# Packing the small constants of a one-core decoder layer, so that its large tiles start elsewhere in the on-chip memory

## The chip, the cores and the metric

The kernel runs on one core of one Trainium2 chip. The metric is the device time of one execution in microseconds; a kernel's time is the median of several executions. The input is one sequence of 1024 tokens of width 1024, all in float32.

## What is computed

One decoder layer with three sublayers, each followed by a layer norm of `alpha * x + sublayer(x)`. The first runs a gated spatial mixer (gMLP) and a latent attention with 16 heads side by side, the second is a cross-attention into 256 memory tokens, the third a mixture of 64 experts of which each token uses two.

```
def hybrid_layer(x, mem, positions, ...):
    proj = x @ w_in + b_in
    u, v, c_q, c_kv, k_rope_raw, gate_gm, gate_mla = jnp.split(proj, IN_SPLITS, axis=-1)
    y_gm = gmlp_branch(gelu(u), gelu(v), ...) @ w_gm_out
    y_mla = mla_branch(c_q, c_kv, k_rope_raw, ...) @ w_mla_out
    merged = sigmoid(gate_gm) * y_gm + sigmoid(gate_mla) * y_mla
    x = layer_norm(DEEPNORM_ALPHA * x + merged @ w_o, ln1_g, ln1_b)
    x = layer_norm(DEEPNORM_ALPHA * x + memory_cross_attention(x, mem, ...), ln2_g, ln2_b)
    y_moe = hierarchical_moe(x, ...)      # (silu(x @ w_gate) * (x @ w_up)) @ w_down, two experts a token
    return layer_norm(DEEPNORM_ALPHA * x + y_moe, ln3_g, ln3_b)
```

## The kernel before

**Products.** Every float32 operand is split into a high part (rounded to the float32r type, by ScalarE) and a low part (the rest, by VectorE), in `split` (lines 109 and 110) or, for the expert weights, in `high` and `low` (lines 1370 and 1379). A product is then three float32r matmuls, high x high, high x low, low x high (`mm3`, lines 124 to 126; `proj_t`, lines 375, 377, 379; `down`, line 1299). Nearly all of them are 128 x 128 weights against 512 moving columns, that is 2048 bytes of each partition for the moving operand and 512 bytes for the weights.

**Stages, in order.** Latents, projections from the input (activation tiles `xT`, `cqT`, `ckvT`; to 540 us); the gMLP output projection (`aT`; to 640); the attention heads (`qT`, `kT`, `pq`, `vT`; to 905); memory keys and values; the merge (`oT`; to 1059); the output projection (`mg`; to 1152); the cross-attention's query projection (`x1T`; to 1245), its heads, and its output projection (`o`; 1297 to 1390); the router; the experts in 32 pairs (from 1443), and the last layer norm. All dense stages use weights from the tile `wsp`. In the experts the moving operand is the weight (`wh`, `wl`), and the stationary one is the token tile `ex` or the hidden tile `ehs`; a pair has 48 matmuls of 512 columns for gate and up and 24 for down. Expert weights come in 1 MB loads (`raw`, line 1237) up to 12 ahead of their use; a load waits until the split of an older tile has freed its buffer.

**Where tiles lie.** Tiles live in pools. Pools on the left side are stacked from the low addresses of a partition up, those on the right side from the high addresses down; each tile takes its bytes rounded up to a multiple of 32. The pool `consts` is the first on the left: its sixteen small tiles (`ident`, `bt`, `gq`, `gkv`, `bs`, `fr`, `rb`, then `i8`, `ip`, `i16`, `i128`, `idv`, `g8`, `up`, `ends`, `ones` of the router) run from byte 16512 to byte 19488, which is 32 past a multiple of 512. All pools of large tiles stand on it: `wsp`, `xT`, `cqT`, `ckvT`, the staging buffers, `ex`, `ehs`, whose sizes are multiples of 512, begin 32 bytes past a multiple of 512. On the right the first pool starts at the top, byte 229344, which is 480 past a multiple of 512: `aT`, `oT`, `x1T`, `o`, `mg`, `x2T`, the query tiles of the cross-attention, the memory tiles, most `raw`, and `wh` and `wl` begin at 480. In the attention, whose pools hold odd sizes, the three buffers of `kT` begin at 32, 64 and 96 and those of `qT` at 64, 96 and 128, so that `qT` is 32 bytes further on than its `kT` each time; `pq` begins at 384.

So a matmul's two operands begin at the same place within 512 bytes in all stages to 540 us; from there on mostly not: one at 480 and the other at 32.

Of the kernel before, what the change touches and what calls it, by code (L numbers as in the profile page):

```python
# [13 lines left out]
F32 = mybir.dt.float32  # L14
FR = mybir.dt.float32r
# [13 lines left out]
NP = NE // 2  # L29
# [38 lines left out]


EARLY = 4  # L70
HOLD = 11


class K:
# [88 lines left out]
    def consts(self):  # L163
        nc, ctx = self.nc, self.ctx
        p = self.cp = ctx.enter_context(self.pool("consts"))
        self.ident = p.tile([128, 128], F32, name="ident")
        make_identity(nc, self.ident)
        self.bt = p.tile([128, 24], F32, name="bt")
        self.gq = p.tile([128, 3], F32, name="gq")
        self.gkv = p.tile([128, 2], F32, name="gkv")  # L170
        self.bs = p.tile([128, 8], F32, name="bs")
        self.fr = p.tile([128, 2], F32, name="fr")
        self.rb = p.tile([72, 1], F32, name="rb")

    def router_consts(self):
        nc, p = self.nc, self.cp
        ts = nc.vector.tensor_scalar

        def iota(n, name, base=0, cm=0, step=1, t=None):
            t = p.tile([128, n], F32, name=name) if t is None else t  # L180
            nc.gpsimd.iota(t, pattern=[[step, n]], base=base, channel_multiplier=cm, allow_small_or_imprecise_dtypes=True)
            return t

        self.i8 = iota(8, "i8", -8)
        self.ip = iota(NP, "ip", -72)
        self.i16 = iota(16, "i16")
        self.i128 = iota(128, "i128")
        self.idv = iota(16, "idv", -2048, 1, 128)
        self.g8 = p.tile([128, 64], F32, name="g8")
        nc.gpsimd.iota(self.g8, pattern=[[1, 8], [0, 8]], base=-8, channel_multiplier=0, allow_small_or_imprecise_dtypes=True)  # L190
        jp = iota(128, "jp", 0, -1, t=self.gp.tile([128, 1024], F32, name="jp", tag="g")[:, :128])

        self.up = p.tile([128, 128], FR, name="up")
        ts(self.up, jp, 0.0, None, op0=ALU.is_gt)
        self.ends = p.tile([NP, NP], FR, name="ends")
        ts(self.ends, jp[:NP, :NP], 0.0, None, op0=ALU.is_ge)
        self.ones = p.tile([128, 128], FR, name="ones")
        ts(self.ones, jp, 0.0, 1.0, op0=ALU.mult, op1=ALU.add)
# [1151 lines left out]
    def first_weights(self):  # L1350
# [3 lines left out]
        self.slots, self.holds = 7 * [self.pb], {}  # L1354
        self.load(EARLY)

# [222 lines left out]
def build(nc, tc, ctx, ins, out, upto=99):  # L1579
# [128 lines left out]
    k.slots = ring[:7] + [k.pa[1]] + ring[7:] + 20 * ring  # L1708
    k.load(HOLD)
    k.pv = k.eps_h.tile([128, 256], F32, name="ph", tag="ph")[:, :NP]  # L1710
# [14 lines left out]
    k.main = k.indices(k.rp, k.rt, k.pv, NP, "x")  # L1725
    k.holds = {HOLD: k.indexed}
    xg = k.gathers()
# [113 lines left out]
```

## Time and profile before

| | |
|---|---|
| Median of 3 executions | 2073.92 us (2072.76 to 2077.05) |
| The profiled execution | 2083.1 us, of which the span from first to last instruction is 2081.3 us |
| TensorE busy | 2004.5 us (96%), 9452 matmuls |
| VectorE, ScalarE, GpSimd busy | 1293.9, 1003.3, 466.1 us |
| Mean granted TensorE clock | 0.98 of full speed |

TensorE is the engine to look at. A matmul's duration in the profile runs from its start to its modelled end, and matmuls overlap: the next starts while the last columns of the one before still drain. What a stream of matmuls costs is therefore the distance from start to start, which is read from the times of start in the timeline; the duration of one is a second sign of it. The timeline merges neighbours of one line; a row's first number is the start of its first instruction.

### The profile page before, as it was taken

Reading aid. Unit: us, or ns where it says so; the run is one execution under the profiler, and the core shown is the slowest. Engines: PE = TensorE matmul, PEld = TensorE weight load, DVE = VectorE, ACT = ScalarE, POOL = GpSimd, SP = SyncE. Lnnn points to the kernel's source line nnn. Section 1 sums busy time; section 2 is a strip of 40 time slices with the busy share of each in tenths; the row PEclk is TensorE's granted clock in tenths of the full one; section 3 lists DMA queues with packets and bytes.
Section 4 is the critical chain, followed back from the end, with each engine's and each line's share of the span. In section 5 each row is a group of like instructions: output and inputs, shape, how many; then the busy total and the mean of one; then the engine's idle time right before and its main releaser. Section 6 shows DMA issues by size and latency. Waiting matters only on the chain.

```text
span 2081.3 us, 25583 instructions
## 1 busy us (share of the span) xinstructions
PE 2004.5 (96%) x9452; PEld 1629.8 (78%) x9452; DVE 1293.9 (62%) x2013; ACT 1003.3 (48%) x1265; POOL 466.1 (22%) x244
## 2 busy tenths in 40 slices
PE   8999999999899999997999999997999999999995
PEld 8888888888687777775888888886788888877872
DVE  5636534341336888743636518477888888877888
ACT  4432423322205777753203316134677777777763
POOL 0002000000101111103002000024355555567742
PEclk9999999999999999999999999997999999999997
DMA  5164953354963665459635703465899999999964
GB/s 179 54 227 162 365 194 133 126 191 147 258 212 94 130 136 129 87 155 250 226 118 185 271 12 113 147 240 201 329 348 375 379 388 388 391 355 364 371 246 189
DMA packets 149321, 461.29 MB, mean 222 GB/s; under 512 B 18301, under 2 KB 64509, under 8 KB 120168
## 3 DMA queue, kind: packets, MB, share of 16 engines
q1 hardware_dynamic: 139608, 442.90, 62.3%
q0 software_dynamic: 9584, 16.70, 2.1%
q8 instruction: 76, 1.25, 0.2%
q14 instruction: 53, 0.43, 0.1%
HBM read 371.16 MB, written 104.73 MB: 229 GB/s over the span
## 4 chain that ended last, share of the span: by engine, by line
PE 88%; DVE 5%; DMA 4%; ACT 1%; issue 1%; POOL 1%; SPq 0%; POOLq 0%; ACTq 0%; DVEq 0%
PE py L1299 8%; PE bank L124 8%; PE bank L126 8%; PE bank L125 8%; PE bank L377 8%; PE bank L375 8%; PE bank L379 8%; PE pg L124 6%; PE pg L126 5%; PE pg L125 5%; PE po L556 2%; PE po L558 2%; PE po L557 2%; PE st L530 1%; PE st L532 1%; PE st L534 1%
## 5 line engine op out<-in xcount | busy, mean ns | idle before, releaser
L1370 ACT ACTIVATE wh<-raw 128x2048 fp32r<-128x2048 f32 (+1 forms) x198 | 361.0, 1857 | 43.8 <-issue 35.3
L1379 DVE TENSOR_TENSOR wl<-raw,wh 128x2048 fp32r<-128x2048 f32 (+1 forms) x166 | 367.7, 2262 | 6.0 <-PE pg L125 4.1
L1379 POOL TENSOR_TENSOR wl<-raw,wh 128x2048 fp32r<-128x2048 f32 x32 | 200.8, 6274 | 244.6 <-ACT wh L1370 244.6
L109 ACT ACTIVATE wsp<-wraw 128x1024 fp32r<-128x1024 f32 (+5 forms) x118 | 111.3, 947 | 243.9 <-PE bank L379 119.6
L124 PE MATMUL pg<-wh,ex 128*128 128x512 f32 x512 | 207.3, 405 | 0.7 <-ACT ex L109 0.7
L125 PE MATMUL pg<-wl,ex 128*128 128x512 f32 x512 | 204.3, 399 | 1.0 <-DVE wl L1379 1.0
L126 PE MATMUL pg<-wh,ex 128*128 128x512 f32 x512 | 204.2, 399 | 0.0
L110 DVE TENSOR_TENSOR wsp<-wraw,wsp 128x1024 fp32r<-128x1024 f32 (+5 forms) x118 | 127.8, 1087 | 98.2 <-ACT wsp L109 96.0
L1299 PE MATMUL py<-wh,ehs 128*128 128x512 f32 x512 | 147.0, 408 | 5.2 <-DVE ehs L110 4.7
L375 PE MATMUL bank<-xT,wsp 128*128 128x512 f32 x384 | 120.1, 390 | 0.0
L377 PE MATMUL bank<-xT,wsp 128*128 128x512 f32 x384 | 119.8, 389 | 0.0
L379 PE MATMUL bank<-xT,wsp 128*128 128x512 f32 x384 | 119.6, 389 | 0.0
L124 PEld LDWEIGHTS pg<-wh,ex 128*128 128x128 f32 x512 | 97.3, 190 | 24.4 <-ACT lgb L1515 1.5
L125 PEld LDWEIGHTS pg<-wl,ex 128*128 128x128 f32 x512 | 97.5, 190 | 23.6 <-DVE wl L1379 1.6
L538 ACT ACTIVATE pe<-st 128x768 f32<-128x768 f32 (+5 forms) x128 | 86.4, 675 | 60.8 <-DVE st L536 60.7
L126 PEld LDWEIGHTS pg<-wh,ex 128*128 128x128 f32 x512 | 97.3, 190 | 23.4
L1299 PEld LDWEIGHTS py<-wh,ehs 128*128 128x128 f32 x512 | 91.8, 190 | 23.6 <-DVE ehs L110 5.8
L719 POOL TENSOR_TENSOR xr<-xr,lb 128x1024 f32<-128x1024 f32 x12 | 28.8, 2402 | 354.6 <-ACT xr L718 354.6
L124 PE MATMUL bank<-wsp,xT 128*128 128x512 f32 (+2 forms) x256 | 91.2, 362 | 6.2 <-ACT wsp L109 6.2
L314 ACT ACTIVATE to<-bank,bt 128x512 f32<-128x512 f32 x48 | 30.4, 684 | 133.6 <-PE bank L379 133.6
L540 ACT ACTIVATE pq<-pe 128x768 fp32r<-128x768 f32 (+5 forms) x128 | 91.3, 713 | 4.1
L125 PE MATMUL bank<-wsp,xT 128*128 128x512 f32 (+2 forms) x256 | 91.8, 359 | 0.0
(396 smaller groups left out, 4648.5 us busy)
## 6 DMA issues: line engine op xcount, KB each, us to landing
raw<-w_gu SPq DMA_DIRECT2D x124, 1024.0 KB
raw<-w_dn SPq DMA_DIRECT2D x62, 1024.0 KB
wraw<-w_t SPq DMA_DIRECT2D x24, 512.0 KB
kn_d<-st SPq DMA_DIRECT2D x8, 1024.0 KB
qn_d<-st SPq DMA_DIRECT2D x8, 1024.0 KB
vv_d<-vt SPq DMA_DIRECT2D x16, 512.0 KB
qT<-qn_d SPq DMA_DIRECT2D x16, 512.0 KB
kT<-kn_d SPq DMA_DIRECT2D x16, 512.0 KB
```

Source lines behind the costliest of these rows:

```text
L109: a = nc.scalar.activation(hi, src, AF.Copy)
L110: (lo_eng or nc.vector).tensor_tensor(lo, src, hi.bitcast(F32), op=ALU.subtract)
L124: mm(out, ah, bh, start=start, stop=False)
L125: mm(out, ah, bl, start=False, stop=False)
L126: mm(out, al, bh, start=False, stop=stop)
L375: mm(ps, wh, x.at(0, kt, h), start=st, stop=False)
L377: mm(ps, wh, x.at(1, kt, h), start=False, stop=False)
L379: mm(ps, wl, x.at(0, kt, h), start=False, stop=sp)
L540: nc.scalar.activation(pq[:, 0, q0:], e[:, q0:], AF.Copy)
L1299: self.nc.tensor.matmul(py[:, q * 512:(q + 1) * 512], hs[:, a, js], w[b][:, j * 1024 + q * 512:j * 1024 + (q + 1) * 512], start=start and ...
L1370: self.nc.scalar.activation(w[0][:, c], self.raws[n][:, c], AF.Copy)
L1379: eng.tensor_tensor(w[1][:, c], self.raws[n][:, c], w[0][:, c].bitcast(F32), op=ALU.subtract)
```

## The change

`bt`, `gq` and `gkv` become slices of one tile of 29 columns, `fr` and `rb` slices of one of 3. A second pool, `consts_r`, is opened on the right side and takes that second tile, `bs`, and the router's small tiles of up to 32 columns (`i8`, `ip`, `i16`, `idv`, `ends`). `consts` then ends at byte 18944, the pools on the right start below byte 228864, and both are multiples of 512.

```
 EARLY = 4
+OFFSET = 0
...
-        self.bt = p.tile([128, 24], F32, name="bt")
-        self.gq = p.tile([128, 3], F32, name="gq")
-        self.gkv = p.tile([128, 2], F32, name="gkv")
-        self.bs = p.tile([128, 8], F32, name="bs")
-        self.fr = p.tile([128, 2], F32, name="fr")
-        self.rb = p.tile([72, 1], F32, name="rb")
+
+        q = self.cq = ctx.enter_context(self.pool("consts_r", side="right"))
+        cols = p.tile([128, 29], F32, name="cols")
+        self.bt, self.gq, self.gkv = cols[:, 0:24], cols[:, 24:27], cols[:, 27:29]
+        self.bs = (q if OFFSET == 0 else p).tile([128, 8], F32, name="bs")
+        cols = q.tile([128, 3], F32, name="colr")
+        self.fr, self.rb = cols[:, 0:2], cols[:72, 2:3]
...
-            t = p.tile([128, n], F32, name=name) if t is None else t
+            t = (self.cq if n <= 32 else p).tile([128, n], F32, name=name) if t is None else t
...
-        self.ends = p.tile([NP, NP], FR, name="ends")
+        self.ends = self.cq.tile([NP, NP], FR, name="ends")
```

No instruction is added or removed, and on every engine and queue the built program has the same instructions in the same order, with the same waits on the same semaphore values; names and addresses differ. Tiles on the left lie 544 bytes lower, those on the right 480 bytes lower. `wsp`, `xT`, `cqT`, `ckvT`, `ex`, `ehs`, `aT`, `oT`, `mg`, `x1T`, `o`, `raw`, `wh` and `wl` now all begin at a multiple of 512. In the attention everything shifts together: `kT` begins at 0, 32 and 64 past a multiple of 512, `qT` at 32, 64 and 96, `pq` at 352.

## Rows read from the trace of the kernel before

**Rows 1.** The page: TensorE's share, and the chain that ended last, by engine.

```profile
PE 2004.5 (96%) x9452; PEld 1629.8 (78%) x9452; DVE 1293.9 (62%) x2013; ACT 1003.3 (48%) x1265; POOL 466.1 (22%) x244
...
PE 88%; DVE 5%; DMA 4%; ACT 1%; issue 1%; POOL 1%; SPq 0%; POOLq 0%; ACTq 0%; DVEq 0%
```

**Rows 2.** Matmuls by tile: count, duration ns min/median/max, first and last start.

```profile
L377 PE MATMUL bank<-xT,wsp x384: 387/389/397, 74.9 to 535.9; 128*128 128x512 f32 x192
...
L375 PE MATMUL bank<-aT,wsp x128: 391/394/628, 536.6 to 639.6; 128*128 128x512 f32 x128
...
L375 PE MATMUL bank<-oT,wsp x100: 394/394/394, 988.9 to 1057.8; 128*128 128x512 f32 x100
...
L125 PE MATMUL bank<-x1T,wsp x128: 392/394/398, 1153.5 to 1244.1; 128*128 128x512 f32 x128
...
L124 PE MATMUL pg<-wh,ex x457: 393/394/628, 1501.2 to 2019.6; 128*128 128x512 f32 x153
```

**Rows 3.** Timeline of TensorE, `cqT` stage: start us, us, what (twelve matmuls apart).

```profile
200.50 0.62 PE L375 MATMUL bank<-cqT,wsp 128*128 128x512 f32 x2
...
203.22 0.62 PE L375 MATMUL bank<-cqT,wsp 128*128 128x512 f32 x2
```

**Rows 4.** Timeline of TensorE, `oT` stage (twelve matmuls apart).

```profile
1040.74 0.63 PE L375 MATMUL bank<-oT,wsp 128*128 128x512 f32 x2
...
1043.54 0.63 PE L375 MATMUL bank<-oT,wsp 128*128 128x512 f32 x2
```

**Rows 5.** Timeline of TensorE, an expert's gate and up (twelve matmuls apart).

```profile
1519.39 0.39 PE L124 MATMUL pg<-wh,ex 128*128 128x512 f32 x1
...
1522.19 0.39 PE L124 MATMUL pg<-wh,ex 128*128 128x512 f32 x1
```

**Rows 6.** Timeline of TensorE, `mg` (nine matmuls apart) and `o` (fifteen apart).

```profile
1070.14 0.40 PE L124 MATMUL bank<-wsp,mg 128*128 128x512 f32 x1
...
1072.24 0.40 PE L124 MATMUL bank<-wsp,mg 128*128 128x512 f32 x1
...
1329.63 0.39 PE L124 MATMUL bank<-wsp,o 128*128 128x512 f32 x1
...
1333.07 0.39 PE L124 MATMUL bank<-wsp,o 128*128 128x512 f32 x1
```

**Rows 7.** Busy us by window: PE, PEld, DVE, ACT, POOL, granted clock, DMA share, GB/s.

```profile
200.00:250.00 50.00, 49.71 (x219) 40.80 (x219) 25.14 (x35) 20.04 (x33) 0.00 (x0) 1.00 1.01 371
...
1200.00:1240.00 40.00, 40.00 (x173) 32.03 (x172) 5.00 (x8) 4.78 (x8) 0.00 (x0) 1.00 0.04 14
...
1500.00:2040.00 540.00, 538.42 (x2461) 432.04 (x2460) 442.45 (x336) 393.00 (x333) 298.37 (x93) 1.00 0.95 362
```

**Rows 8.** The chain in order of time: start us, us, what; merge, experts' start and pairs.

```profile
971.11 9.64 DMA ri<-rinv_d
...
1447.62 6.53 DVE wl L1379
...
1515.35 4.20 PE py L1299 x18
...
1533.47 4.19 PE py L1299 x18
...
2028.13 4.21 PE py L1299 x18
```

**Rows 9.** Waits from 1500 to 2040 us: us in total, times, longest.

```profile
ACT wh L1370 <- issue: 33.6, 27, 2.3
...
SPq L1237 <- DVE wl L1379: 318.3, 135, 6.6
```

**Rows 10.** ScalarE copies of one size, by form: count, busy us, mean ns.

```profile
L109 ACT ACTIVATE wsp<-wraw 128x1024 fp32r<-128x1024 f32 x90 | 94.9, 1059 | 218.1 <-PE bank L379 105.4 <-PE bank L126 81.9 <-DMA wraw<-w_gmo 15.3
...
L540 ACT ACTIVATE pq<-pe 128x1024 fp32r<-128x1024 f32 x16 | 17.0, 1060 | 0.5
```

**Rows 11.** Attention matmuls by form, 690 to 850 us: count, busy us, mean ns.

```profile
L532 PE MATMUL st<-qT,kT 96*128 96x512 f32 x59 | 21.6, 394 | 0.0
```

## The prediction

> **What bounds the kernel now.** I read the page first: TensorE is busy 96% of the span, and 88% of the chain that ended last is its matmuls; VectorE holds 5% and DMA 4% [rows 1]. So time can only go where matmuls get shorter or where TensorE waits. The change gives nobody less to do and moves no wait; only start addresses differ. The question is whether any duration in the trace depends on an address.
>
> I then looked at one and the same kind of matmul (128 x 128 weights, 512 columns) in different stages. With `xT` as moving operand its median is 389 ns; with `aT`, `oT` and `x1T` it is 394, and 394 again in the experts [rows 2]. The distance from start to start tells more. In the `cqT` stage twelve matmuls take 203.22 - 200.50 = 2.72 us, 226.7 ns each [rows 3]. In the `oT` stage, same lines of code, twelve take 1043.54 - 1040.74 = 2.80 us, 233.3 ns each [rows 4], and in the experts 1522.19 - 1519.39 = 2.80 us, again 233.3 [rows 5]. At full clock, 2.4 GHz, 512 columns are 213.3 ns; the two kinds lie 13.3 and 20.0 ns above, 32 and 48 clocks.
>
> What differs between the kinds? Not traffic: the quick window from 200 to 250 us has DMA at full share and VectorE half busy, and the slow one from 1200 to 1240 has DMA at 0.04 and VectorE at 5 us of 40 [rows 7]. Not the clock, 1.00 in both. Not the code: lines 375 to 379 run in both. Not high addresses: `cqT` lies in the same upper part of the memory as `aT`. What goes with it is the place within 512 bytes. `xT`, `cqT` and `wsp` all begin at 32; `aT`, `oT`, `x1T`, `wh`, `wl` begin at 480 while their weights begin at 32. With the moving operand at 32 and the weights at 480 it is in between and changes: `mg` has 2.10 us for nine in its first half, 233.3 ns, and `o` 3.44 us for fifteen, 229.3 [rows 6]. I take it that the moving read and the load of the next weights, which run at the same time, meet in the memory two or three times per matmul, 16 clocks each, depending on how far apart their addresses are within 512 bytes. That reading is a guess; that distance zero goes with 226.7 ns is what the rows show.
>
> **A rule that speaks against it.** By the Trainium skill, "TensorE: Matmul & The Clock Gate", step-by-step part of "What happens when you issue a matmul", moving operand and weight load have read ports of their own, so that loading the next weights takes nothing from the running matmul. By that rule the distance of the two addresses could not matter and the change would be worth 0 us; the 6.7 ns between rows 3 and 4 would need another cause, and I found none in the trace. It stands below as the rival of no change.
>
> **The change part by part.**
>
> *Packing and the second pool.* The same loads and iotas write to other places: 0 us. Their readers take a column of a wider tile. Nothing waits longer, since every wait is the same.
>
> *Stages to 540 us.* Distance zero before and after; both operands move from 32 to 0. I take no change. Bounds: one meeting of 16 clocks (6.7 ns) more or less per matmul, worked out with the rivals.
>
> *Attention, 640 to 905 us.* All its tiles move by the same 32 bytes, so that distances stay. Its 512-column matmuls average 394 ns now [rows 11], I expect the same. 0 us.
>
> *Dense stages from 540 us.* 6.7 ns saved per matmul wherever TensorE is what bounds. `aT`: 3 x 128 = 384 [rows 2], less the first 48, which come while their activations are still being loaded: 336 x 6.7 = 2.2 us. `oT`: in the first part of the merge the chain goes through loads (9.64 us at once [rows 8]), so only the matmuls after 988.5 us count, three lines of some hundred [rows 2]: 300 x 6.7 = 2.0. `x1T`: 384 x 6.7 = 2.6. `mg`: half of 384 at 6.7 and half like `o` at 2.6 [rows 6]: 1.8. `o`: 384 x 2.6 = 1.0. Sum 9.6 us.
>
> *Experts.* From 1515.35 us to 2028.13 the chain is one pair after the other, 28 steps, most of them 18.1 us (1533.47 - 1515.35) [rows 8]. In a pair lie 72 matmuls of 512 columns: 72 x 6.7 = 0.48 us, 28 x 0.48 = 13.4. Ahead of that the chain runs through VectorE (6.53 us of `wl` at once [rows 8]) and I count nothing for it.
>
> Who comes late next there? TensorE is busy 538.4 of 540 us, VectorE 442, ScalarE 393 [rows 7]: a pair of 17.6 us still has room for them. DMA has a share of 0.95, which would become 0.95 x 18.1 / 17.6 = 0.98. That is near its end, but the loads are paced by VectorE, which frees the buffers (318.3 us of waits in the queue [rows 9]), not by bandwidth, and ScalarE waits before `wh` only 33.6 us, 27 times, on something that the profile doesn't name [rows 9]. If DMA can't follow, the up to 12 loads ahead cover the first pairs, and the worst is the gain lost, not time added.
>
> *ScalarE, VectorE, DMA.* A ScalarE copy of 128 x 1024 takes 1060 ns on `pq`, which begins at 384, and 1059 on `wsp`, at 32 [rows 10]: no effect, 0 us. For DMA the trace has no pair to compare. By the Trainium skill, "DMA: Bandwidth & Descriptors", "How a descriptor splits into AXI transactions", a piece that doesn't start at a multiple of 256 bytes costs a transaction more: 33 for 32 with 8 KB rows. Were it so for these writes, I estimate at most 3% of the 4% of the chain that is DMA, 2.5 us gained; no run so far shows it, and it is not in the sum.
>
> Sum: 9.6 + 13.4 = 23.0 us. The profiled execution took 2083.1 us, span 2081.3; less 23.0 that is 2060.1. The median, 2073.92, lies 9.2 below that execution, so I predict 2073.9 - 23.0 = 2050.9, say 2051.
>
> **The rivals.**
>
> *Only part of it.* The spacing is not a property of the pair alone: `mg` shows 233.3 with the addresses that in `o` give 229.3 [rows 6], so a stream can stay in a slow rhythm that it entered after a break, and the experts have a break (transposes) every 12 matmuls or so. If half of the streams stay slow, the gain is 11.5 us: 2062. Against it: the dense stages at distance zero have breaks too and show 389 as their median, 397 as their longest [rows 2].
>
> *No change.* Another cause than the distance goes with the stages. For it: the rule above, and that no row shows the same tile at two addresses. Time 2074.
>
> *More than that.* Starts at a multiple of 512 may spare meetings that starts at 32 still have: 13.3 ns over 213.3 remain in rows 3. One meeting less, 6.7 ns, on all matmuls at distance zero: some 1,940 before 540 us (1152 of them of `xT`, 3 x 384 [rows 2]) and some 4,000 after, 39 us on top: 2012. In the experts DMA, already at 0.95, would take back part, so rather 2025 to 2035.
>
> *Slower.* The quick rhythm is seen only where both operands begin 32 bytes into a 512-byte piece. Starting both exactly on a boundary could make the two reads meet once more, at their common start. It decides if that costs the 16 clocks: then the stages to 540 us go from 226.7 to 233.3, 1,940 x 6.7 = 13 us and some 2.5 us for the shorter matmuls of the latents, while the later stages, already at 233.3, gain nothing: 2074 + 15.5 = 2089. Against it: in the attention, where the operands begin at other places again and 32 bytes apart, the average is 394 ns [rows 11], what 480 and 32 give, and nothing worse than that is seen anywhere.
>
> **How the numbers follow.** Forecast as summed (2046 to 2056): 0.66. Only part (2056 to 2066): 0.11. More: 0.08. No change: 0.09. Slower: 0.06. A measurement of this kernel can tell about 0.2%, 4 us, from no change. Faster by more: 0.66 + 0.11 + 0.08 = 0.85; same 0.09; slower 0.06. The range runs from 2038, which takes in the nearest part of "more" and the DMA estimate, to 2066, and leaves out no change, slower and the far part of "more", together 0.2.
>
> **What would show it.** Right: twelve matmuls in `oT`, `x1T` and in the experts' gate and up 2.72 us apart instead of 2.80, medians of 389 instead of 394, a pair of 17.6 us instead of 18.1, and the stages to 540 us and the attention as they were. Wrong: 2.80 us still in the late stages (no change), 2.80 in the `cqT` stage (slower), spacings under 226 ns (more), or shorter matmuls with a pair still at 18.1 us, which would mean that another engine or DMA bounds it.

## The result and the profile after

The changed kernel takes 2056.1 us (median of 4 executions, 2053.92 to 2057.21), the kernel before 2074.6 us beside it (2072.76 to 2077.05): a ratio of 0.9909, 95% interval 0.9892 to 0.9926, 18.5 us less. On a second chip it was 2057.0 against 2078.8 us, 0.9904 (0.9882 to 0.9925). Forecast were 2051 us and a range of 2038 to 2066: the sign, the stages and the cause that was named (how far apart the two operands of a matmul start) held, the gain was 18.5 instead of 23.0 us.

The profiled execution of the changed kernel took 2056.15 us, that is its median; the one of before lay 9 us above its own. The two spans, 2081.3 and 2054.1, must therefore not be subtracted. What follows compares stages and single distances.

The page, first TensorE's and the other engines' busy time, then the chain that ended last, beside [rows 1]:

```profile
PE 1980.4 (96%) x9452; PEld 1628.3 (79%) x9452; DVE 1293.7 (63%) x2013; ACT 1003.4 (49%) x1265; POOL 469.2 (23%) x244
...
PE 88%; DMA 4%; DVE 4%; ACT 1%; issue 1%; POOL 1%; SPq 0%; POOLq 0%; DVEq 0%; ACTq 0%
```

The same 9452 matmuls, and TensorE has the same 96% of the span and 88% of the chain: its busy time is 24 us shorter, and that of each other engine is within 3.1 us of what it was. The bound has not moved.

Matmuls by tile (count, duration in ns least/median/most, first and last start; lines stand one or two further down than before), beside [rows 2]:

```profile
L377 PE MATMUL bank<-xT,wsp x384: 389/389/476, 73.1 to 534.2; 128*128 128x512 f32 x192
...
L377 PE MATMUL bank<-aT,wsp x128: 389/389/792, 535.3 to 635.0; 128*128 128x512 f32 x128
...
L377 PE MATMUL bank<-oT,wsp x128: 389/389/632, 949.1 to 1052.3; 128*128 128x512 f32 x128
...
L125 PE MATMUL bank<-x1T,wsp x128: 389/389/477, 1145.7 to 1234.1; 128*128 128x512 f32 x128
...
L125 PE MATMUL pg<-wh,ex x512: 389/389/632, 1420.9 to 1997.5; 128*128 128x512 f32 x171
```

The stages that had 394 now have 389, what `xT` had all along and has still. The distance from start to start says it more sharply. Timeline of TensorE (start us, us, what), `cqT`, `oT`, the experts' gate and up, `mg` and `o`, each pair of rows twelve matmuls apart, beside [rows 3 to 6]:

```profile
199.22 0.61 PE L377 MATMUL bank<-cqT,wsp 128*128 128x512 f32 x2
...
201.94 0.61 PE L377 MATMUL bank<-cqT,wsp 128*128 128x512 f32 x2
...
1030.27 0.61 PE L377 MATMUL bank<-oT,wsp 128*128 128x512 f32 x2
...
1032.99 0.61 PE L377 MATMUL bank<-oT,wsp 128*128 128x512 f32 x2
...
1521.00 0.39 PE L125 MATMUL pg<-wh,ex 128*128 128x512 f32 x1
...
1523.72 0.39 PE L125 MATMUL pg<-wh,ex 128*128 128x512 f32 x1
...
1065.63 0.39 PE L125 MATMUL bank<-wsp,mg 128*128 128x512 f32 x1
...
1068.35 0.39 PE L125 MATMUL bank<-wsp,mg 128*128 128x512 f32 x1
...
1320.19 0.39 PE L126 MATMUL bank<-wsp,o 128*128 128x512 f32 x1
...
1322.91 0.39 PE L126 MATMUL bank<-wsp,o 128*128 128x512 f32 x1
```

2.72 us in all five, 226.7 ns a matmul. Before, it was 2.72 in `cqT` alone and 2.80 in `oT` and the experts; `mg` and `o` had 233.3 and 229.3 ns a matmul in the rows shown [rows 6].

The chain in order of time through the experts, beside [rows 8]:

```profile
1516.37 4.11 PE py L1301 x18
...
1534.11 4.11 PE py L1301 x18
```

A pair takes 17.74 us instead of 18.12; 17.6 was forecast. Nobody else came late (busy us by window, and waits, beside [rows 7, 9]):

```profile
1500.00:2010.00 510.00, 508.60 (x2376) 416.94 (x2375) 426.94 (x321) 380.58 (x320) 291.67 (x92) 1.00 0.95 366
...
ACT wh L1372 <- issue: 28.0, 25, 2.1
...
SPq L1239 <- DVE wl L1381: 298.6, 131, 6.5
```

TensorE is busy 508.6 of 510 us, and the loads still wait for VectorE to free their buffers. The DMA share of 0.95 in this window and in that of before is an average that takes in the end of the stage, when all loads have come. Over the same eighteen pairs, first before, then after:

```profile
1515.10:1841.00 325.90, 325.90 (x1514) 264.72 (x1513) 271.33 (x201) 243.21 (x198) 172.64 (x56) 1.00 0.99 379
```

```profile
1498.40:1817.60 319.20, 319.20 (x1516) 264.54 (x1513) 271.20 (x201) 243.49 (x198) 170.58 (x56) 1.00 1.00 387
```

TensorE has no idle time in either. DMA's share was 0.99 already and is 1.00 now, at 387 instead of 379 GB/s.

One group went the other way. Matmuls of 256 columns with `memT` as moving operand, first before, then after:

```profile
L124 PE MATMUL bank<-memT,wsp x64: 276/276/415, 904.9 to 928.9; 128*128 128x256 f32 x64
```

```profile
L126 PE MATMUL bank<-memT,wsp x64: 283/283/579, 902.5 to 926.8; 128*128 128x256 f32 x64
```

From start to start they went from 113.6 to 120.0 ns, at full clock, and the 192 of `mk` from 117.5 to 119.6: together 192 x (6.4 + 2.1) ns = 1.6 us lost. That is worked out from the spacings; the stretch from the first `memT` matmul to `oT` waits for loads too (46 to 49 us from kernel to kernel), and its length does not show the loss.

### The profile page after: what moved, and what is told of

It reads as the page before. It is cut to its first block, busy times and chain, and to the rows that moved or that the text cites. A ratio compares the mean times of both kernels' runs of the same rounds, so it can differ in the third digit from the quotient of the medians.

```text
span 2054.1 us, 25583 instructions
## 1 busy us (share of the span) xinstructions
PE 1980.4 (96%) x9452; PEld 1628.3 (79%) x9452; DVE 1293.7 (63%) x2013; ACT 1003.4 (49%) x1265; POOL 469.2 (23%) x244
## 3 DMA queue, kind: packets, MB, share of 16 engines
q1 hardware_dynamic: 139608, 442.90, 62.2%
## 4 chain that ended last, share of the span: by engine, by line
PE 88%; DMA 4%; DVE 4%; ACT 1%; issue 1%; POOL 1%; SPq 0%; POOLq 0%; DVEq 0%; ACTq 0%
PE bank L125 9%; PE bank L126 8%; PE bank L127 8%; PE py L1301 8%; PE bank L379 8%; PE bank L381 8%; PE bank L377 8%; PE pg L125 6%; PE pg L127 6%; PE pg L126 6%; DMA kT<-kn_d 2%; PE po L558 2%; PE po L560 2%; PE po L559 2%; PE st L532 1%; PE st L534 1%
## 5 line engine op out<-in xcount | busy, mean ns | idle before, releaser
L1381 DVE TENSOR_TENSOR wl<-raw,wh 128x2048 fp32r<-128x2048 f32 (+1 forms) x166 | 363.2, 2236 | 4.5 <-PE pg L126 2.8
L1381 POOL TENSOR_TENSOR wl<-raw,wh 128x2048 fp32r<-128x2048 f32 x32 | 202.6, 6332 | 229.3 <-ACT wh L1372 229.3
L110 ACT ACTIVATE wsp<-wraw 128x1024 fp32r<-128x1024 f32 (+5 forms) x118 | 111.2, 947 | 237.8 <-PE bank L381 123.4
L125 PE MATMUL pg<-wh,ex 128*128 128x512 f32 x512 | 204.0, 398 | 0.7 <-ACT ex L110 0.7
L127 PE MATMUL pg<-wh,ex 128*128 128x512 f32 x512 | 201.1, 393 | 0.0
L316 ACT ACTIVATE to<-bank,cols 128x512 f32<-128x512 f32 x48 | 30.4, 685 | 133.7 <-PE bank L381 133.6
L542 ACT ACTIVATE pq<-pe 128x768 fp32r<-128x768 f32 (+5 forms) x128 | 91.4, 714 | 4.1
```

The lines of the kernel that those rows point to most:

```text
L110: a = nc.scalar.activation(hi, src, AF.Copy)
L125: mm(out, ah, bh, start=start, stop=False)
L127: mm(out, al, bh, start=False, stop=stop)
L542: nc.scalar.activation(pq[:, 0, q0:], e[:, q0:], AF.Copy)
L1381: eng.tensor_tensor(w[1][:, c], self.raws[n][:, c], w[0][:, c].bitcast(F32), op=ALU.subtract)
```

## Experiments: is it the distance, the boundary, or the packing?

Four kernels were timed beside the kernel before on one chip. All are the changed kernel with unused bytes put below the large tiles of one side or both, so that packing, pools and order of work stay and the starts move. To make room, all four also drop the table `g8`, which nothing reads, with the GpSimd instruction that fills it, and give the attention's `sums` one buffer; among the four nothing but the starts differs. `PADL` and `PADR` are bytes on the left and on the right side; the edit below is the first kernel's, and the others have 224 and 32, 288 and 0, 256 and 256:

```
+PADL, PADR, PADA = 288, 32, (0, 0)
...
         self.fr, self.rb = cols[:, 0:2], cols[:72, 2:3]
+        if PADR:
+            q.tile([128, PADR // 4], F32, name="padr")
...
-        self.g8 = p.tile([128, 64], F32, name="g8")
-        nc.gpsimd.iota(self.g8, pattern=[[1, 8], [0, 8]], base=-8, channel_multiplier=0, allow_small_or_imprecise_dtypes=True)
...
         self.ones = p.tile([128, 128], FR, name="ones")
+        if PADL:
+            p.tile([128, PADL // 4], F32, name="padl")
...
-            sums = sm.tile([128, 128], F32, name="sums")
+            sums = sm.tile([128, 128], F32, name="sums", bufs=1)
```

**Back to the old places, 32 and 480.**

> The packed kernel, with 288 bytes of padding on the left side and 32 on the right, so that large tiles begin 32 bytes into a 512-byte piece on the left and at 480 on the right, as in the kernel before; the packing and the moved constants stay. (In this and the next three, the table g8, which nothing reads, and its iota on GpSimd are dropped and the sums of the attention have one buffer, to make room.) If the distance of the two operands within 512 bytes is the cause: oT, x1T and the experts back at 233.3 ns from matmul to matmul, a pair of experts 18.1 us, about 2074 us. If the start at a multiple of 512 is the cause: 2074 us too. If the packing or the order of the loads brought the gain: 226.7 ns in oT, a pair of 17.7 us, about 2056 us.

Measured: 2077.1 against 2077.4 us, ratio 0.9997 (0.9983 to 1.0011). The gain is gone, and the pair is back at 18.10 us (chain in order of time):

```profile
1508.82 4.19 PE py L1304 x18
...
1526.92 4.20 PE py L1304 x18
```

So the packing and the order of the small loads are worth nothing that the time shows; the gain hangs on where large tiles start.

One stage did not go back. `mg` had 233.3 ns in its first 264 matmuls before (nine in 2.10 us [rows 6]); here it has 228.9 from its start, nine in 2.06 us:

```profile
1070.09 0.40 PE L127 MATMUL bank<-wsp,mg 128*128 128x512 f32 x1
...
1072.15 0.39 PE L127 MATMUL bank<-wsp,mg 128*128 128x512 f32 x1
```

The places within 512 bytes are the same in both kernels, and both come into `mg` from `oT` without a break. So at 64 bytes apart the places alone do not fix the spacing: before, the stream kept the slower one until its first break, at 1121 us, and had 228.9 ns from there on.

**Both sides at 480.**

> Large tiles begin at 480 within 512 bytes on both sides: no multiple of 512, but distance zero between moving operand and weights. If the distance alone matters: 226.7 ns in oT and x1T, 17.7 us for a pair of experts, about 2056 us as with the change. If the start at a multiple of 512 matters: 233.3 ns in oT and x1T, a pair of 18.1 us, about 2074 us, and the stages up to 540 us, where both sides were at 32 and then at 0, may be slower too.

Measured: 2057.0 us, ratio 0.9897 (0.9869 to 0.9926), as with the change; the pair takes 17.72 us:

```profile
1515.16 4.11 PE py L1304 x18
...
1532.88 4.11 PE py L1304 x18
```

No tile starts at a multiple of 512 here, and nothing is lost. What the change aimed at, a start at a multiple of 512, is not what brings the time; that both operands start alike is.

**32 bytes apart instead of 64.**

> Left side at 32, right side at 0: the moving operand lies 32 bytes below the weights in aT, oT, x1T and the experts, and 32 above them in mg and o, where the kernel before had 64. If any distance but zero costs 16 clocks more: 233.3 ns in oT and x1T and 18.1 us for a pair, about 2074 us. If the cost is in pieces of 64 bytes (distance 32 counts as none): 226.7 ns, 17.7 us, about 2056 us. If the multiple of 512 on the moving side matters alone: 226.7 in the experts and oT, 233.3 in the stages before 540 us, where both lie at 32.

Measured: 2082.0 us, ratio 1.0015 (1.0001 to 1.0029), the pair 18.13 us:

```profile
1515.21 4.20 PE py L1304 x18
...
1533.34 4.20 PE py L1304 x18
```

Moving operands at a multiple of 512 with weights 32 bytes off gain nothing. `mg` and `o`, which had 232.0 and 229.0 ns on average at +64, have 233.3 at +32: 384 x (1.3 + 4.3) ns = 2.2 us of the 3.1 (by the ratio) to 4.5 us (by the medians) that the kernel is slower than before; where the rest lies is not shown.

**Half a piece apart, 0 and 256.**

> Left side at 0, right side at 256: the operands lie half a 512-byte piece apart. If the period is 512 bytes and only distance zero is quick: 233.3 ns or more in oT, x1T and the experts, about 2074 us or more. If the period is 256 bytes or less: 226.7 ns, a pair of 17.7 us, about 2056 us. If reads half a piece apart never meet: under 226.7 ns, and under 2056 us.

Measured: 2057.0 us, ratio 0.9891 (0.9866 to 0.9915), the pair 17.75 us:

```profile
1502.52 4.11 PE py L1304 x18
...
1520.27 4.11 PE py L1304 x18
```

256 bytes are as good as none: the period is 256, not the 512 on which change and prediction rested. But for `mg` with the old places, the distances of all four agree with that stage by stage (mean from start to start in ns, matmuls of 512 columns at full clock, worked out from the starts in the traces):

| moving / weights | before | old places | 32 apart | both 480 | 256 apart | after |
|---|---|---|---|---|---|---|
| `xT` / `wsp` | 227.1 | 227.1 | 227.1 | 227.1 | 227.1 | 227.1 |
| `x1T` / `wsp` | 233.3 | 233.3 | 233.3 | 226.8 | 226.8 | 226.8 |
| `wsp` / `mg` | 232.0 | 228.9 | 233.3 | 226.8 | 226.8 | 226.8 |
| `wsp` / `o` | 229.0 | 229.0 | 233.3 | 227.0 | 226.9 | 226.9 |
| `wh` / `ex` | 233.3 | 233.3 | 233.5 | 227.7 | 228.1 | 228.1 |
| `wh` / `ehs` | 233.0 | 233.0 | 233.4 | 228.5 | 228.8 | 228.8 |

## Experiments: the cost of a distance by itself

**Streams with the moving operand shifted.** Just before the last `xT` projection, streams of matmuls are added whose operands are slices of two `xT` tiles; `c` is a shift in columns of 4 bytes, and two transposes stand before each stream as a break.

```
+            for r in range(reps):
+                a, b = move(r), 128 * (r % 4) + load(r)
+                mm(ps[:, :n], w[:, b:b + 128], x[:, a:a + n], start=r == 0, stop=r == reps - 1)
...
+        for c in (*range(0, 128, 4), 1, 2, 3, 126, 127):
+            stream(512, 24, lambda r: c, lambda r: 0)
```

> The changed kernel with streams of matmuls added just before the last xT projection, whose results nobody reads: 24 matmuls of 512 columns each (moving operand from one xT tile, weights from another, both tiles at a multiple of 512 bytes), the moving operand shifted by 0, 16, 32 ... 496 bytes and by a few steps of 4 bytes, a break of two transposes before each stream; then the same with 256 columns in steps of 32 bytes; then streams in which the weights, or the moving operand, take turns at distance 0 and 64; then one that goes from distance 0 to 64 in its middle. Added work about 260 us. If only distance zero and 256 are quick: 226.7 ns from start to start at shifts 0 and 256, 229 to 233.3 at all the others. If the two reads meet in pieces of 64 bytes: 226.7 ns also at 16 and 240 bytes. If some distance avoids the meetings altogether: about 213 to 220 ns there, and the kernel could gain more. With 256 columns, if the rows of memT are right: 120 ns at distance zero and 113 to 114 at some others. If it is the load of the next weights that meets the running matmul, a stream whose weights take turns at 0 and 64 takes turns too, 226.7 and about 230 ns.

Timeline, one row for each stream of 24, at shifts of 0, 16, 32, 64, 240 and 256 bytes, then with 256 columns at 0 and 32:

```profile
525.87 5.74 PE L320 MATMUL bank<-xT,xT 128*128 128x512 f32 x24
531.59 5.80 PE L320 MATMUL bank<-xT,xT 128*128 128x512 f32 x24
537.36 5.85 PE L320 MATMUL bank<-xT,xT 128*128 128x512 f32 x24
...
548.92 5.76 PE L320 MATMUL bank<-xT,xT 128*128 128x512 f32 x24
...
612.77 5.92 PE L320 MATMUL bank<-xT,xT 128*128 128x512 f32 x24
618.66 5.74 PE L320 MATMUL bank<-xT,xT 128*128 128x512 f32 x24
...
740.32 3.12 PE L320 MATMUL bank<-xT,xT 128*128 128x256 f32 x24
743.41 3.04 PE L320 MATMUL bank<-xT,xT 128*128 128x256 f32 x24
```

The mean of the last twelve distances of each stream, in ns; shifts of 256 to 496 bytes give the same again within 0.1:

| shift, bytes | 0 | 16 | 32 | 48 | 64 | 80 | 96 | 112 |
|---|---|---|---|---|---|---|---|---|
| ns | 226.7 | 231.7 | 233.3 | 230.0 | 228.9 | 231.1 | 233.3 | 231.1 |

| shift, bytes | 128 | 144 | 160 | 176 | 192 | 208 | 224 | 240 |
|---|---|---|---|---|---|---|---|---|
| ns | 231.7 | 233.3 | 234.3 | 233.3 | 233.3 | 234.6 | 233.3 | 236.7 |

These are the kernel's own numbers: -64 (192) gives the 233.3 of the experts and of `x1T` before, +64 the 228.9 that `o` had. Two more things are seen. At shift 0 the stream does not begin at 226.7: its distances after the break are 229, 233, 236, 224, 231, 236, 228, 233, 231, 226, and only then 227 for good. And 256 columns behave otherwise: 120.0 ns at shift 0, 116.7 at 32. That has the sign of the loss in `memT`, and its 120.0 after the change; the 113.6 that `memT` had before, with the moving operand 64 bytes below the weights, were met at none of the sixteen shifts (117.8 at 192), and that stays open. The streams in which one operand takes turns at 0 and 64 run through a pattern of eight distances between 225 and 240 ns, 232 on average, and don't take turns; which load meets which matmul is not told by them.

**More places, and both operands shifted.** Every multiple of 4 bytes, equal shifts of both operands, weights shifted alone, fewer weight columns, other column counts, by the same helper.

> More streams of the same kind, added at the same place of the changed kernel, whose results nobody reads: the moving operand at every multiple of 4 bytes up to 252 with the weights at 0; both operands shifted by the same 4, 8, 16, 32, 64 and 128 bytes; the weights alone shifted by 4 to 252 bytes; the moving operand 4 bytes below weights that are themselves at 32, 64 and 128; weights of 96, 64 and 32 columns; and 384, 320 and 128 moving columns. If the distance alone decides: 226.7 ns for every equal shift; weights alone 4 bytes further give what the moving operand 4 bytes below gave, 226.7; and the experts with their weights at 4 (232 ns) would be a riddle. If the place of the weights within their own 16 or 32 bytes counts too: equal shifts by 4 and 8 bytes are slower than 226.7, those by 32 and more are not, and weights shifted alone by 4 bytes give about 232. If the 13.3 ns that stay above 213.3 at distance zero are meetings with the load of the weights: fewer weight columns bring it down, to about 220 ns with 64. If some multiple of 4 bytes is better than zero: below 226.7 ns there.

Timeline, one row a stream of 24: both operands at 4, 8, 16, 32 and 64 bytes; then the weights alone at 4:

```profile
759.55 5.95 PE L320 MATMUL bank<-xT,xT 128*128 128x512 f32 x24
765.48 5.80 PE L320 MATMUL bank<-xT,xT 128*128 128x512 f32 x24
771.25 5.85 PE L320 MATMUL bank<-xT,xT 128*128 128x512 f32 x24
777.07 5.72 PE L320 MATMUL bank<-xT,xT 128*128 128x512 f32 x24
782.76 5.71 PE L320 MATMUL bank<-xT,xT 128*128 128x512 f32 x24
...
794.15 5.82 PE L320 MATMUL bank<-xT,xT 128*128 128x512 f32 x24
```

Settled, that is 237.8, 231.1, 233.3, 226.7, 226.7 and 232.3 ns. Equal starts are enough at 32, 64 and 128 bytes (whole tiles of this kernel start at multiples of 32), and not at 4, 8 and 16. Of the 64 places of the moving operand with weights at 0, five reach 226.7 ns: 0, 28, 60, 156 and 252 bytes. None is under it, the worst are 240.0 (100, 132 and 244). At 28 and 60 the stream needs no matmul to settle (319, then 227, 227, 226). Weights of 64 columns instead of 128 don't bring the floor down: 230.0 ns at shift 0, 228.3 at 64 bytes; and with 96 columns it is 32 and 240 bytes that reach 226.7, while shift 0 has 230.0. So the best place hangs on the shape of the weights too, and the 13.3 ns above 213.3 are not a share of a weight load that gets smaller with it; what they are stays open.

## Experiments: can the rest be had?

The pair stayed at 17.73 instead of 17.6 us. The next four kernels ran side by side on one chip.

**The change once more,** as their measure.

> The changed kernel once more, as the measure for the three beside it on the same chip: about 0.991 of the kernel before.

Measured: 2057.0 us, ratio 0.9904 (0.9882 to 0.9925).

**Both edits at once, then each alone.** The experts' activations, the weights of their matmuls, 4 bytes further (for room, `g8` is dropped here too); and `qT` reserved ahead of `vT`.

```
-        x = self.ep.tile([128, 2, 1024], FR, name="ex", tag="ex", bufs=1)
+        x = self.ep.tile([128, 2056], FR, name="ex", tag="ex", bufs=1)[:, 1:2049].rearrange("p (k n) -> p k n", k=2)
...
-        hs = self.ep.tile([128, 2, 256], FR, name="ehs", tag="ehs")
+        hs = self.ep.tile([128, 576], FR, name="ehs", tag="ehs")[:, 1:513].rearrange("p (k n) -> p k n", k=2)
...
             self.kts.append(kt)
+            self.qts.append(one.tile([97, 2, 1024], FR, name=f"qT{b}"))
...
-            self.qts.append(one.tile([97, 2, 1024], FR, name=f"qT{b}"))
```

> The edits of the next two runs together: the experts' weights 4 bytes off, and qT level with kT in the attention. If both theories below hold: 2.2 us less from the experts and about 1.5 to 2 us less from the attention than with the change alone, about 2052 to 2053 us. If only one holds: about 2054. If neither: about 2056 us.

> As with the change, but the experts' activations (ex, ehs: the weights of their matmuls) begin 4 bytes behind a multiple of 256, so that the moving operand lies 4 bytes below the weights; their tiles are made a little larger for that, and the table g8, which nothing reads, is dropped with its iota. In the separate streams both distances end at 226.7 ns, but distance zero needs 10 matmuls after a break and loses 40 ns, distance -4 only 5 and loses 14. If the experts fell short of 17.6 us for a pair because each of the three breaks of a pair is paid anew: 3 x 26 = 78 ns less for each pair, 17.65 instead of 17.73 us, 28 x 0.078 = 2.2 us less in all, about 2054 us. If the shortfall has another cause (an engine or DMA that paces the pairs): 17.73 us as before and about 2056 us, whatever the spacings do.

> As with the change, but in the attention each tile qT is reserved ahead of vT, so that it begins at the same place within 512 bytes as its kT (32 bytes apart before). If the distance rules there too: the matmuls of st<-qT,kT with 512 columns go from 232 to about 227 ns from start to start, 288 + 96 of them by 5 ns, 1.9 us less where TensorE paces the attention, about 2054 us; those with 256 columns 119 to 120. If what paces the attention is ScalarE's exponentials or VectorE: shorter matmuls, but the same time, about 2056 us.

Measured: both 2069.6 us, 0.9956 (0.9942 to 0.9970); the experts' edit alone 2071.7, 0.9969 (0.9954 to 0.9983); `qT` alone 2056.9, 0.9901 (0.9882 to 0.9921).

The experts' edit is a miss: it loses 14.7 of the gain, and the pair goes to 18.05 us:

```profile
1505.28 4.18 PE py L1299 x18
...
1523.33 4.19 PE py L1299 x18
```

The reason was the theory that the distance alone decides: -4 had been measured with the moving operand at 508 bytes (252 within 256) and the weights at 0, and the edit had the moving operand at 0 and the weights at 4. The experts showed 232.4 ns, and the separate stream at just these places, measured afterwards, 232.3. A pair took 0.312 us more, 8.7 us over 28 pairs. The two profiled executions, 2069.6 and 2055.4 us, differ by 2.3 us more in the experts' first three pairs and by 3.4 in the `oT` stage, which varies by as much among the other kernels. So the place of the operands moves the experts in either direction, and the step to 17.65 us is not shown by this edit: it changed the resting distance too.

`qT` level with `kT` changed nothing: 232.8 ns instead of 232.0 for `st<-qT,kT` with 512 columns. The attention's streams are 3 to 6 matmuls long, of changing size and tile, and end before a stream at shift 0 has settled. That suggested one more edit, in which `qT` stands 28 bytes behind `kT`:

```
+            self.qts.append(one.tile([97, 2056], FR, name=f"qT{b}")[:, 7:2055].rearrange("p (k n) -> p k n", k=2))
```

> As the attention edit before, but each qT begins 28 bytes behind the place of its kT; in the separate streams that place needs no matmul to settle (227, 226, 227 from the second matmul on), distance zero needs ten. If the short streams of the attention stayed at 232 ns at distance zero because they end before they settle: 227 to 228 ns now for st<-qT,kT with 512 columns, 288 x 4 to 5 ns, 1 to 1.5 us less, about 2055 us. If 97 rows or 65 columns, other shapes than in the separate streams, follow another rule: 231 to 233 ns as before and about 2057 us. If loads to a start that is no multiple of 64 bytes cost more: longer waits on qT<-qn_d ahead of the attention's matmuls.

Measured: 2058.6 us, ratio 0.9906 (0.9872 to 0.9941), no difference from the change. `st<-qT,kT` went from 232.0 to 230.6 ns; mean durations in the attention, by form, with the change and then with this edit:

```profile
L536 PE MATMUL st<-qT,kT 96*128 96x512 f32 x96 | 35.2, 394 | 0.0
```

```profile
L536 PE MATMUL st<-qT,kT 96*128 96x512 f32 x94 | 34.3, 391 | 0.0
```

So a place that settles at once helps these short streams by about a third of what was expected, and 288 x 1.4 ns = 0.4 us is nothing that the kernel's time can show. No version was found that beats the changed kernel. Moving the experts' `wh` and `wl` to 28 bytes would need their eight tiles to grow by 256 bytes each; that was not tried.

## Why the prediction was right, and where it was short

**What bounds the kernel, and what the chain would follow.** Right. TensorE stayed at 96%, and each stage shrank by its matmuls.

**The cause.** Right in kind: the distance of the two operands' starts sets the time of a matmul, and undoing it alone gives the whole gain back. The rival of no change falls: with the same instructions, 64 bytes more under the left side (both at 480 against the old places) turn 226.8 into 233.3 ns in `x1T`. By the Trainium skill, "TensorE: Matmul & The Clock Gate", step-by-step part of "What happens when you issue a matmul", the two operands have read ports of their own and the weight load takes nothing from the running matmul; what the prediction drew from it, that the distance could not matter, does not hold here. The prediction was wrong in the period, 256 and not 512 bytes, and too simple in two ways: below 32 bytes the weights' own place counts, and at 64 bytes apart `mg` had either of two spacings. That it is the load of the next weights that meets the moving read was called a guess, and is one still: that the weights' address matters is shown (weights alone shifted by 32, 64 or 128 bytes: 232.9 to 233.3 ns), what meets is not. The weight loads themselves are as long after as before, 1628.3 and 1629.8 us busy.

**Stages to 540 us and the attention.** Right: 226.7 ns in `cqT` and 232 in the attention, unchanged. The rival *slower* (a boundary as common start costs one meeting more) and the rival *more* (it spares one) both fall by the `xT` row of the table: 227.1 at 32, at 0 and at 480.

**Dense stages, 9.6 us.** About right as a sum, in part by luck. From the first matmul of a stage to the first of the next, before and after, and with the old places and the change once more as a second pair:

| stage | forecast gain | before, after | old places, change again |
|---|---|---|---|
| `aT` | 2.2 | 105.6, 102.2 | 105.5, 102.6 |
| `oT` | 2.0 | 105.6, 104.3 | 105.8, 103.1 |
| `mg` | 1.8 | 94.2, 92.3 | 93.1, 92.3 |
| `x1T` | 2.6 | 91.4, 89.1 | 91.4, 89.1 |
| `o` | 1.0 | 94.5, 93.7 | 94.5, 93.7 |

The gains of the first pair are 3.4, 1.3, 1.9, 2.3 and 0.8, 9.7 us in all. `oT` waits for loads and takes 100 to 108 us from kernel to kernel whatever the places are, so that its own term is not measured; `aT` gained more than 384 x 6.6 ns = 2.5 us, and stretches at 1.2 GHz of different length (10.2 us before, 6.8 after, between 549 and 562 us) lie in that stage; the second pair has 10.2 us in both, and `aT` gains 2.9. The term for `mg` took it for granted that half of that stage is slow; with the old places none of it is, and the second pair gains 0.8.

**The shorter matmuls of `memT` and `mk`, left out.** This is the first step that failed: the prediction took 512 columns as the pattern for all, and priced nothing for 384 matmuls of 256 columns after 900 us. By their spacings they lost 1.6 us.

**The experts, 13.4 us.** The second, and the larger: the term is 28 pairs x 72 x 6.7 ns, and a pair gained 0.373 instead of 0.48 us. Sixteen pairs one after the other, from 1515 us before and from 1516 us after, show where it stayed. The 72 matmuls of a pair stand in three streams, with breaks for transposes between them; in ns from start to start:

| of a pair | before | after | gained in a pair |
|---|---|---|---|
| first and last distance of each stream (6) | 946 + 702 in all | 945 + 698 in all | 5 |
| second to eleventh, where the stream is that long (24) | 233.2 each | 229.5 each | 88 |
| the others (42) | 233.3 each | 226.7 each | 279 |
| the pair (means, rounded) | 18107 | 17733 | 373 |

So 42 of 72 got what was forecast, the 24 behind a break about half, the 6 beside a break nothing. Behind a break the experts' distances run 231, 236, 228, 232, 231 and then 227 ns; they have settled after six or seven, the separate stream at shift 0 after ten. 28 x 0.373 = 10.4 us, and along the chain the 28 steps gained 10.3.

The rival *only part of it* named that mechanism, slow streams behind a break, and was off in its size (half of all) as the forecast was (none). The step that failed is the argument against that rival: it went by durations (389 as median, 397 as longest), which hardly show the slow start, and not by the starts. The trace of before has it, in the stages where both operands were at the same place already. Timeline before, an `xT` stream that begins at 525.59 behind four transposes:

```profile
526.14 0.63 PE L377 MATMUL bank<-xT,wsp 128*128 128x512 f32 x2
...
528.45 0.62 PE L375 MATMUL bank<-xT,wsp 128*128 128x512 f32 x2
...
531.17 0.62 PE L375 MATMUL bank<-xT,wsp 128*128 128x512 f32 x2
```

Ten matmuls soon behind the break take 2.31 us, 231 ns each, and the next twelve 2.72, 226.7 each. An estimate from these rows: 0.04 us lost at the start of each of a pair's two long streams, and nothing gained on the six distances beside a break (6 x 6.7 ns), leave 0.36 us of the 0.48; 0.373 was measured.

**Ahead of the 28 pairs, 0 us.** The first three pairs were counted as nothing, because the chain goes through VectorE there. They took 59.4 us before and 57.0 after (59.5 and 57.0 in the second pair of kernels). Some 1.1 us of that are three times 0.373. The rest goes with the clock: a stretch of 3.4 us at 1.2 GHz lies there before and with the old places, behind 2.3 us in which TensorE waited, and none in the change or the change once more, though TensorE waited 2.4 us there after the change too. The kernel 32 bytes apart, with slow matmuls, the same wait and no such stretch, takes 57.9. So that part is luck and not the change.

**Put together.** The profiled executions of the old places and of the change once more lie within 2 us of their medians, so that their spans can be compared: 2073.2 and 2053.4 us, 19.8 less. The dense stages gained 9.5 of it, the 28 pairs 10.4, the first three pairs 2.5, and all that lies between lost 2.6, 2.2 of it from the end of `aT` to the start of `oT`. So the forecast of 23.0 is too high by the 3 us of the experts' term, and of the two things left out one gained about what the other lost. That 9.7 + 10.4 - 1.6 gives just the 18.5 us between the medians is chance.

**DMA.** The forecast was that it can follow, at a share of 0.98, and that its writes might get cheaper by 2.5 us at most, outside the sum. It followed; but the 0.95 that the forecast started from was the average with the end of the stage in it, and over the same eighteen pairs the share went from 0.99 to 1.00 (the rows above). The queue's line of the page, before and after (packets, MB, time of its packets as a share of 16 engines' span):

```profile
q1 hardware_dynamic: 139608, 442.90, 62.3%
```

```profile
q1 hardware_dynamic: 139608, 442.90, 62.2%
```

62.3% of 2081.3 is 1296.7 us, 62.2% of 2054.1 is 1277.6: the same packets took 1.5% less time. Worked out in the same way it is 1297.8 with the old places, 1290 to 1293 with 480 on both sides and with 32 bytes apart, and 1277 to 1282 in the change once more, with 0 and 256, with `qT` level and with both edits. But the experts' edit alone, most of whose loads land at multiples of 256 too, has 1290. By the Trainium skill, "DMA: Bandwidth & Descriptors", "How a descriptor splits into AXI transactions", a piece of 8 KB that doesn't start at a multiple of 256 bytes takes a transaction more. The sign agrees, the size is half of the 3% estimated from it, and with that one kernel the cause is not shown. What of it reached the chain is not told apart here; with 480 on both sides the kernel is as quick as with 0.

## What to carry to other kernels

When the same matmul shows two spacings in one trace, compare the start addresses of its two operands before anything else: here up to 6.7 ns in 233, on some 4,200 of 9452 matmuls, came from moving operand and weights that started at different places within 256 bytes, and equal places (0, 32, 64, 128 and 480 were tried) cured it for weights of 128 columns. Read the distance from start to start, not durations alone, and cost such a gain per stream, not per matmul: the first six to ten distances after a break got about half of it, those beside a break nothing. Look for the settling in a stage that has the good places already. And price matmuls of other sizes apart: those of 256 columns lost where those of 512 gained.

## What was not expected

- A stream with both operands at the same place takes up to ten matmuls or so to come to rest (229, 233, 236, 224, 231 ... 226.7 ns; six or seven in the experts), one with the moving operand 28 or 60 bytes further none.
- At 64 bytes apart one and the same stage, `mg`, ran at 233.3 ns in one kernel and at 228.9 in another with the same places.
- The weights' place within 32 bytes counts by itself: both operands at 4 bytes 237.8 ns, both at 32 bytes 226.7.
- With 256 columns equal places are among the worse ones, 120.0 ns against 116.7 at 32 bytes.
- No place among the 64 tried gives 512 columns in less than 226.7 ns, 544 clocks at 2.4 GHz.
